# Gate and up projections of paired feed-forward tiles by Strassen's seven products

## The chip, the cores and the metric

The kernel runs on one core of a Trainium2 chip. The core has a matrix engine (PE, with its weight loads shown apart as PEld), a vector engine (DVE), a scalar engine (ACT), a general engine (POOL, which also issues DMAs that add while they write) and a queue engine (SP) that issues the plain DMAs. The metric is the device time of one execution in microseconds; of several executions the median is given.

## The reference

A trunk of two layers over 1024 tokens of width 1024. Layer 0 mixes tokens with a causal convolution module, layer 1 with a causal pooling mixer over windows of 2, 4, 8 and 16 tokens. After each mixer comes a SwiGLU feed-forward of width 2816, and the part that the change touches is its first half:

```
def swiglu_ffn(h, w_gate, w_up, w_down):
    return (jax.nn.silu(h @ w_gate) * (h @ w_up)) @ w_down

h = modulate(rms_norm(x, norm_ffn_g[i]), sh_f, sc_f)
x = x + (1.0 + g_f)[:, None, :] * swiglu_ffn(h, ...)
```

Everything is float32. Shift, scale and gate vectors (the "ada" vectors) come from a product of a conditioning vector with a large matrix for each layer.

## The kernel before, in words

The activations are kept transposed: channels on the 128 partitions, tokens along the free axis. The 1024 tokens are two chunks, A (`ch.i` 0) and B (`ch.i` 1), of 512 tokens. There are therefore four feed-forwards: A and B of layer 0, A and B of layer 1. Each works in 22 tiles `f` of 128 hidden channels.

**Precision.** A float32 factor is split into a high part, rounded to the matrix engine's float32r format, and a low part, the rest. `products` (L406) multiplies high by high, high by low and low by high: three matmuls for each 128 x 128 weight block, each with its own weight load, adding into one PSUM bank. The high part of a weight is an ACT copy of a raw tile that SP's DMA brought (`load_weight`, L391). For the low part ACT writes the negated high part into the second half of the tile and a DMA of POOL's queue adds the raw weight to it from memory. So each weight is fetched twice, and DVE has nothing to do with it.

**Feed-forward.** `ffn_p1` (L790) makes one tile: for gate, then for up, 8 blocks x 3 matmuls of 512 columns; then ACT takes silu of the gate, DVE multiplies with up, ACT casts the high part and DVE or POOL subtracts for the low part. `ffn_p2` (L815) makes the down products of two tiles: for each of 8 output tiles 2 x 3 matmuls, and DVE adds the result, times the gate vector, into the residual `x` (`update`). `ffn` (L827) puts these units in order: a down unit runs after the first tile of the next pair. The last feed-forward ends in `ending` (L844), which makes the down products in two halves of 256 tokens, so that the last norm can start early.

**Order.** PE runs in the order in which the program is written. The other engines are put in order by a list scheduler at compile time, from priorities and estimated times. Background work (the taps of the convolution, norms, the pooling mixer, the layer-1 ada vectors) is written as tasks; `pace` (L175) emits steps of them between matmuls by an estimated clock for each engine, with lower priority than the direct work, and `finish` (L187) emits all that is left of a task where its result is needed. `either` (L141) picks DVE or POOL for an operation by these clocks and the price list `PRICES`.

**Weights.** `run_units` (L526) holds a queue of all weights in order of use and loads ahead as long as fewer than `W_BUFS` = 5 are held. A weight tile is 128 x 2 x 1024 (high and low side by side), and raw weights have 3 buffers.

**Buffers.** `slot` (L227) gives the high and low parts of normalised activations, 16 for each chunk. `wslot` (L231) gives wider tiles, 8 for each chunk; the feed-forward puts its hidden activations in there. `temp` (L252) gives scratch tiles. PSUM has 6 rotating banks and 2 spare ones.

**Around the change.** `with_pool` (L1051) lays the layer-1 pooling of chunk A under the layer-0 feed-forward of B, and the pooling of B under the layer-1 feed-forward of A. It starts the task `pool` at one unit, and at a later unit it waits for it (`need`), emits the pool products (`pool_out`) and starts the norm for the next feed-forward. `final_a`, the last norm of chunk A, runs under the last feed-forward.

Of the kernel before, what the change touches and what calls it, by code (L numbers as in the profile page):

```python
# [16 lines left out]
P = 128  # L17
# [17 lines left out]
GROUP = 2  # L35
W_BUFS = 5
RAW_BUFS = 3
ADA_BUFS = 2
# [8 lines left out]
STRETCH = 1.35  # L47
LATER = 300
DELAY = {"stats": 2.75, "spread": 1.5}
DELAY_BEHIND = {"stats": 8, "spread": 4}  # L50
# [52 lines left out]
def trunk(ctx, tc, xT, c, vec, ada, adan, w1, w2, wgu, wdn, wpl, out):  # L103
# [11 lines left out]

    def matmul(out, lhsT, rhs, start, stop):
        n = out.shape[-1]
        clock["PE"] += n / 2400 * (1 if rhs.dtype == F32R else 4) + 0.0025
        last_mm[0] = nc.tensor.matmul(out, lhsT, rhs, start=start, stop=stop).ins.name  # L119

# [270 lines left out]
    def load_weight(src, n=D, load=nc.sync.dma_start, summed=False):  # L391
        raw = raws.tile([P, D], F32, tag="raw", name=nm("raw"))[:, :n]
        dst = raw if len(src.shape) == 2 else raw.rearrange("p (a b) -> p a b", a=src.shape[1])
        load(dst, src)
        wt = wts.tile([P, 2, D], F32R, tag="w", name=nm("w"))
        S_.copy(wt[:, 0, :n], raw)
        if summed:
            S_.activation(wt[:, 1, :n], raw, AF.Copy, scale=-1.0)
            low = wt[:, 1, :n]
            order(nc.gpsimd.dma_start(low if len(src.shape) == 2 else low.rearrange("p (a b) -> p a b", a=src.shape[1]), src, accum_op=ADD))  # L400
            clock["G"] = max(clock["G"], clock["PE"]) + 1.0
            return wt
        either(n).tensor_tensor(wt[:, 1, :n], raw, wt[:, 0, :n].bitcast(F32), op=SUB)
        return wt

    def products(out, wt, k, act, first, last, o=0, n=None):  # L406

        wk = slice(k * P, (k + 1) * P)
        for i, (wp, a) in enumerate(((0, 0), (0, 1), (1, 0))):
            cols = act[a][:, o : o + n] if n else act[a]  # L410
            matmul(out, wt[:, wp, wk], cols, start=first and i == 0, stop=last and i == 2)

# [113 lines left out]
    def run_units(cap, early):  # L526

        queue = [w for ws, _ in units for w in ws]
        loaded = list(early)
        del queue[: len(early)]  # L530
        used = [0]

        def ahead(free):
            while queue and len(loaded) + used[0] - free < cap:
                loaded.append(load_weight(queue.pop(0), summed=True))
                if len(loaded) > 1:
                    break

        for ws, emit in units:
            def take():  # L540
                ahead(0)
                used[0] += 1
                return loaded.pop(0)
            emit(take)
            used[0] -= len(ws)
            ahead(0)
            pace()
# [278 lines left out]

    def ffn(ch, l, pick, at_end=False):  # L827

        us, pend = [], None
        ends = [NF - n for n in range(0, NF, GROUP)][::-1]  # L830
        if NF % GROUP == 1:
            ends[0] += 1
        for f0, f1 in zip([0] + ends, ends):
# [8 lines left out]
        return us  # L842

    def ending(ch, l, fs):  # L844
# [88 lines left out]
    for k in range(KT + 1):  # L933
        if k < KT:
            w = wts.tile([P, 2, D], F32, tag="w", name=nm("adaw"))
            load_next(w, ada_m[0, k][:, 0:2, :])
            ada_dot(w[:, 1], 0, 1, k)
            tc.add_manual_dep(V_.last.ins, t_last if k else rstd_last, edge, reason="behind the first norm")
# [7 lines left out]
        if k < KT:  # L946
            ada_dot(w[:, 0], 0, 0, k)
            V_.tensor_scalar(scale_m[:, k : k + 1], mod[:, KT + k : KT + k + 1], scale_b[:, k : k + 1], V("norm_mix_g", k), op0=ADD, op1=MUL)
# [101 lines left out]

    def with_pool(us, ch, at, out_at):  # L1051

        for i, (e, ws) in enumerate(us):
            if i == at:
                if ch.i == 0:
                    ada_need((1, 0), (1, 1), (1, 2))
                put(("pool", ch.i), lambda: pool(ch))
            if i == out_at:
# [63 lines left out]
```

## Time and profile before

| what | value |
|---|---|
| median of 3 runs | 1887.41 us (1884.03 to 1890.82) |
| span of the profiled execution, first to last instruction | 1887.1 us |
| busy, share of the span: PE / DVE / ACT / POOL | 96% / 52% / 51% / 34% |
| matmuls on PE | 8104 |
| bytes moved by DMA | 382.31 MB |

The page of the profile gives no separate time of the profiled execution beside its span; the span lies 0.3 us under the median. In the rows of the views, a line number such as L97 or L119 is that of a helper through which all operations of an engine go (L97 for DVE, ACT and POOL, L119 for matmuls), so the names say more than the lines: "gate<-hhi,w" writes the tile `gate` from `hhi` and `w`. In a group row the count stands after x, then the total in us, the mean of one in ns, and the idle time before them with its cause. Durations of matmuls overlap; the distance between their starts is what one costs in a row of many.

### The profile page before, as it was taken

How to read it: one execution, taken by the hardware profiler on the slowest of the kernel's cores; microseconds unless marked ns; L12 is line 12 of the kernel's file. 1: busy time of each engine (PE TensorE's matmuls, PEld its weight loads, DVE VectorE, ACT ScalarE, POOL GpSimd, SP SyncE). 2: the span in 40 equal slices, each digit the busy share in tenths (PEclk: the TensorE clock that was granted, in tenths of full speed). 3: DMA queues.
4: the chain of work that ended last, by engine and by line, in shares of the span. 5: the costliest groups of instructions: out<-in, count | busy, mean ns of one | idle time of the engine just before them, and what ended most of it. 6: DMA issues, size and time to landing. Idle time of an engine off the chain costs nothing.

```text
span 1887.1 us, 21837 instructions
## 1 busy us (share of the span) xinstructions
PE 1803.9 (96%) x8104; PEld 1465.9 (78%) x8104; DVE 985.5 (52%) x1512; ACT 969.5 (51%) x1246; POOL 634.1 (34%) x675
## 2 busy tenths in 40 slices
PE   6899839999999999999999999999999999999996
PEld 4666628788888887888888888888888888888885
DVE  7778872898986326475742224643522243322225
ACT  3655645866666554554454444545544444344443
POOL 3478742687762211264211111321111111111111
PEclk9999969999999999999999999999999999999998
DMA  7968836889798897999978787887887879888782
GB/s 251 296 193 227 211 65 158 206 208 244 199 235 205 210 236 175 249 251 278 270 183 207 173 197 189 194 195 186 189 198 180 198 179 251 179 199 200 180 192 66
DMA packets 115292, 382.31 MB, mean 203 GB/s; under 512 B 11889, under 2 KB 22257, under 8 KB 115186
## 3 DMA queue, kind: packets, MB, share of 16 engines
q0 software_dynamic: 43488, 158.35, 46.0%
q1 hardware_dynamic: 70544, 221.51, 34.6%
q8 instruction: 64, 1.05, 0.2%
q10 hardware_dynamic: 1154, 1.05, 0.2%
q14 instruction: 42, 0.34, 0.1%
HBM read 376.67 MB, written 4.19 MB: 202 GB/s over the span
## 4 chain that ended last, share of the span: by engine, by line
PE 87%; DMA 6%; DVE 5%; issue 1%; ACT 1%; POOL 0%; SPq 0%; DVEq 0%; ACTq 0%
PE dn L119 24%; PE gate L119 24%; PE up L119 23%; PE y L119 6%; DMA adaw<-in_adan_dram 3%; PE a L119 3%; PE g L119 3%; PE first L119 2%; DMA adaw<-in_ada_dram 2%; DVE adaw L97 1%; PE ada L119 1%; DVE x L97 1%; DVE t L97 1%; DVE acc L97 1%; DMA w<-in_wdn_dram 1%
## 5 line engine op out<-in xcount | busy, mean ns | idle before, releaser
L97 ACT CAST w<-raw 128x1024 fp32r<-128x1024 f32 x312 | 326.0, 1045 | 512.0 <-issue 293.9
L119 PE MATMUL gate<-hhi,w 128*128 128x512 f32 x1408 | 451.1, 390 | 0.5 <-DVE x L97 0.5
L119 PE MATMUL up<-hhi,w 128*128 128x512 f32 x1408 | 451.4, 390 | 0.0
L119 PE MATMUL dn<-ghi,w 128*128 128x512 f32 (+1 forms) x1440 | 447.2, 387 | 2.2 <-ACT ghi L97 1.2
L400 POOL DMA_DIRECT2D w<-in_wgu_dram x176 | 154.5, 878 | 760.7 <-ACT w L97 739.0
L97 DVE SCALAR_TENSOR_TENSOR x<-dn,gains,x 128x512 f32<-128x512 f32 (+1 forms) x360 | 261.7, 735 | 119.0 <-PE dn L119 118.7
L97 ACT ACTIVATE w<-raw 128x1024 fp32r<-128x1024 f32 x302 | 319.0, 1056 | 0.0
L119 PEld LDWEIGHTS dn<-ghi,w 128*128 128x128 f32 x1440 | 268.7, 188 | 61.5 <-ACT ghi L97 1.6
L97 DVE TENSOR_TENSOR t<-t,up 128x512 f32<-128x512 f32 x88 | 60.4, 686 | 485.5 <-PE up L119 465.1
L119 PEld LDWEIGHTS gate<-hhi,w 128*128 128x128 f32 x1408 | 264.3, 188 | 56.5 <-DVE x L97 1.0
L119 PEld LDWEIGHTS up<-hhi,w 128*128 128x128 f32 x1408 | 264.3, 188 | 54.7
L119 PE MATMUL dn<-glo,w 128*128 128x512 f32 (+1 forms) x720 | 279.4, 388 | 1.6 <-POOL glo L97 1.6
L119 PE MATMUL gate<-hlo,w 128*128 128x512 f32 x704 | 274.4, 390 | 1.1 <-DVE hlo L97 1.1
L119 PE MATMUL up<-hlo,w 128*128 128x512 f32 x704 | 273.9, 389 | 0.0
L97 POOL TENSOR_TENSOR pa<-pa,pr 128x512 f32<-128x512 f32 x172 | 244.4, 1513 | 19.7 <-ACT pr L97 16.6
L97 DVE SCALAR_TENSOR_TENSOR ca<-u,vecs,ca 128x512 f32<-128x512 f32 x276 | 188.9, 746 | 0.2
L119 PEld LDWEIGHTS dn<-glo,w 128*128 128x128 f32 x720 | 135.5, 188 | 30.0 <-POOL glo L97 1.9
L119 PEld LDWEIGHTS gate<-hlo,w 128*128 128x128 f32 x704 | 132.2, 188 | 29.3 <-DVE hlo L97 1.9
L400 POOL DMA_DIRECT2D w<-in_wdn_dram x88 | 78.2, 889 | 225.3 <-ACT w L97 223.3
L119 PEld LDWEIGHTS up<-hlo,w 128*128 128x128 f32 x704 | 132.2, 188 | 27.2
L97 ACT ACTIVATE t<-gate 128x512 f32<-128x512 f32 x88 | 52.2, 593 | 161.5 <-PE gate L119 155.0
L97 DVE SCALAR_TENSOR_TENSOR adaw<-adaw,cact 128x1024 f32<-128x1024 f32 x64 | 108.4, 1695 | 43.8 <-DMA adaw<-in_ada_dram 42.0
(123 smaller groups left out, 1734.2 us busy)
## 6 DMA issues: line engine op xcount, KB each, us to landing
raw<-in_wgu_dram SPq DMA_DIRECT2D x176, 512.0 KB, 7.1
w<-in_wgu_dram POOLq DMA_DIRECT2D x176, 512.0 KB, 8.0
raw<-in_wdn_dram SPq DMA_DIRECT2D x88, 512.0 KB, 5.4
w<-in_wdn_dram POOLq DMA_DIRECT2D x88, 512.0 KB, 9.4
adaw<-in_ada_dram SPq DMA_DIRECT2D x48, 512.0 KB, 7.5
raw<-in_w_dram SPq DMA_DIRECT2D x44, 512.0 KB, 6.5
w<-in_w_dram POOLq DMA_DIRECT2D x34, 512.0 KB, 8.4
adaw<-in_adan_dram SPq DMA_DIRECT2D x32, 512.0 KB, 5.6
```

The lines of the kernel that those rows point to most:

```text
L97: self.last = self.order(getattr(self.eng, name)(out, *args, **kw))
L119: last_mm[0] = nc.tensor.matmul(out, lhsT, rhs, start=start, stop=stop).ins.name
L400: order(nc.gpsimd.dma_start(low if len(src.shape) == 2 else low.rearrange("p (a b) -> p a b", a=src.shape[1]), src, accum_op=ADD))
```

## The change

In three of the four feed-forwards (B of layer 0, A and B of layer 1), the first two tiles stay as they were. After them come tiles in pairs up to `UNTIL` = (14, 14, 20), and the rest (8, 8 and 2 tiles) as before.

For a pair of tiles `f`, `f+1` the product of the 256 x 1024 weights with the 1024 x 512 activations is cut into halves along all three axes: two tiles, the front and back four channel blocks, and the left and right 256 tokens. That would be 8 quarter products; Strassen's scheme (in Winograd's form) makes it 7 of sums and differences of quarters. An object `Pair` stands for gate or up of such a pair.

- `combined` makes the four sums of activation quarters once for each feed-forward, as a task, with high and low parts, in the other chunk's `slot` tiles.
- `Pair.load` fetches the two raw weights once. `Pair.prepare` makes three plain quarters and four sums, each with high part (ACT) and low part (DVE, or `either`); sums lie in the other chunk's `wslot` tiles. It has a priority of its own, `PREPARED`.
- `ffn_pair` emits seven `quad`s of 4 blocks x 3 matmuls of 256 columns into two PSUM banks. ACT and DVE read a bank between quads that add into the same bank. It prepares the next object midway.
- `Downs` makes the down products of two tiles for 4 of the 8 output tiles, one after every second quad; its weights are fetched once, in halves, and their low parts are subtracted on DVE or POOL.
- Weight tiles are now 9 tiles of 128 x 1024 (high and low each take one), raw tiles 4. `run_units` counts a weight as 2 and a `Pair` as 4 of these 9. In the very first stage two ada loads of 512 KB stand for one of 1024 KB.
- `pooled` starts the pooling task only after the pairs, and needs it at unit `OUT_AT` = 7 of the rest.

```diff
-W_BUFS = 5
-RAW_BUFS = 3
+W_BUFS = 9
+RAW_BUFS = 4
+PREPARED = 120
+UNTIL = (14, 14, 20)
+OUT_AT = 7
...
-        wt = wts.tile([P, 2, D], F32R, tag="w", name=nm("w"))
-        S_.copy(wt[:, 0, :n], raw)
+        hi, lo = (wts.tile([P, D], F32R, tag="w", name=nm("w"))[:, :n] for _ in range(2))
+        S_.copy(hi, raw)
...
+    def combined(ch):
+        other = chunks[1 - ch.i]
+        h = st["h", ch.i]
+        got = st["T", ch.i] = []
+        for k in range(KT // 2):
+            whole = []
+            for hi, lo in (h[k], h[k + KT // 2]):
+                t = window(ch.n, "hf")
+                either(ch.n).tensor_tensor(t, f32(hi), f32(lo), op=ADD)
+                whole.append(t)
+            a, b = whole
+            q12, q34 = temp(ch.n, "tf"), temp(ch.n, "tf")
+            V_.tensor_tensor(q12[:, LEFT], a[:, LEFT], a[:, RIGHT], op=SUB)
+            V_.scalar_tensor_tensor(q12[:, RIGHT], q12[:, LEFT], -1.0, b[:, RIGHT], op0=MUL, op1=SUB)
+            V_.tensor_tensor(q34[:, LEFT], b[:, RIGHT], a[:, RIGHT], op=SUB)
+            V_.scalar_tensor_tensor(q34[:, RIGHT], q12[:, RIGHT], -1.0, b[:, LEFT], op0=MUL, op1=SUB)
+            yield
+            row = []
+            for q in (q12, q34):
+                hi, lo = slot(other, "thi"), slot(other, "tlo")
+                S_.copy(hi, q)
+                V_.tensor_tensor(lo, q, f32(hi), op=SUB)
+                row += [(hi[:, LEFT], lo[:, LEFT]), (hi[:, RIGHT], lo[:, RIGHT])]
+            got.append(row)
+            yield
...
+        def prepare(self):
...
+            with tc.high_priority(offset=-PREPARED):
+                w11 = plain(a11, V_)
+                s1 = temp(QUAD, "acc", 2)
+                V_.tensor_tensor(s1, a21, a22, op=ADD)
+                e1 = summed(s1)
+                s2 = temp(QUAD, "ny", 2)
+                V_.tensor_tensor(s2, s1, a11, op=ADD)
+                e2 = summed(s2)
+                w12 = plain(a12, V_)
+                s3 = temp(QUAD, "acc", 2)
+                V_.tensor_tensor(s3, a11, a21, op=ADD)
+                e3 = summed(s3)
+                s4 = temp(QUAD, "ny", 2)
+                V_.tensor_tensor(s4, s2, a12, op=ADD)
+                e4 = summed(s4)
+                w22 = plain(a22, V_)
...
+    def quad(out, w, acts, first):
+        for k, act in enumerate(acts):
+            cols = slice(k * P, (k + 1) * P)
+            for i, (wp, a) in enumerate(((0, 0), (0, 1), (1, 0))):
+                matmul(out, w[wp][:, cols], act[a], start=first and k + i == 0, stop=k == len(acts) - 1 and i == 2, skip_group_check=True)
...
+    def ffn_pair(ch, l, me, following, downs, later):
...
+            quad(a[:, :H], w11, b11, True)
+            S_.copy(r[:, LEFT], a[:, :H])
+            quad(right, s1, t1, True)
+            S_.copy(q[:, RIGHT], right)
+            pace()
+            down()
+            quad(a[:, :H], s2, t2, False)
+            S_.copy(r[:, RIGHT], a[:, :H])
+            if following is not None and hasattr(following, "raws"):
+                following.prepare()
+            quad(left, w12, b21, False)
+            pace()
+            down()
+            quad(a[:, :H], s3, t3, False)
+            V_.tensor_tensor(q[:, RIGHT], q[:, RIGHT], a[:, :H], op=ADD)
+            quad(right, s4, b22, False)
+            V_.tensor_tensor(r, r, e, op=ADD)
+            if later is not None:
+                later.load(later.dps[0])
+            pace()
+            down()
+            quad(a[:, :H], w22, t4, False)
...
-    fb_, fa_, last = ffn(B, 0, True), ffn(A, 1, True), ffn(B, 1, True, at_end=True)
-    with_pool(fb_[:-1], A, 3, 14)
-    with_pool(fa_[:1] + fb_[-1:] + fa_[1:-1], B, 5, 17)
-    for i, (e, ws) in enumerate(last[:1] + fa_[-1:] + last[1:]):
-        if i == 3:
-            put("final_a", lambda: final(A))
-        unit(e, *ws)
+    before, pairs, rest = ffn_mixed(B, 0, UNTIL[0])
+    put(("T", 1), lambda: combined(B))
+    add(before)
+    paired(B, pairs)
+    pooled(rest[:-1], A, OUT_AT)
+    before, pairs, rest_a = ffn_mixed(A, 1, UNTIL[1])
+    add(before[:1] + rest[-1:])
+    put(("T", 0), lambda: combined(A))
+    add(before[1:])
+    paired(A, pairs)
+    pooled(rest_a[:-1], B, OUT_AT)
+    before, pairs, rest = ffn_mixed(B, 1, UNTIL[2], True)
+    add(before[:1] + rest_a[-1:])
+    put(("T", 1), lambda: combined(B))
+    add(before[1:])
+    put("final_a", lambda: final(A))
+    paired(B, pairs)
+    add(rest)
```

`ffn_mixed` lays out one such feed-forward: the two plain tiles, the pairs with their `Downs`, the left-over `Downs` as units of their own (`alone`) between the first tiles of the rest, and the rest from `ffn`.

More of the change, by code (lines that the diff above doesn't have):

```diff
@@ L410, in products @@
             cols = act[a][:, o : o + n] if n else act[a]
-            matmul(out, wt[:, wp, wk], cols, start=first and i == 0, stop=last and i == 2)
+            matmul(out, wt[wp][:, wk], cols, start=first and i == 0, stop=last and i == 2)
     def rsqrt(v, y, t):
@@ L531, in run_units, with ahead @@
         used = [0]
-        def ahead(free):
-            while queue and len(loaded) + used[0] - free < cap:
-                loaded.append(load_weight(queue.pop(0), summed=True))
+        cost = lambda w: 4 if isinstance(w, Pair) else 2
+        def ahead():
+            held = sum(cost(w) for w in loaded) + used[0]
+            while queue and (held + cost(queue[0]) <= cap or not loaded):
+                w = queue.pop(0)
+                held += cost(w)
+                loaded.append(w.load() if isinstance(w, Pair) else load_weight(w, summed=True))
                 if len(loaded) > 1:
```

185 lines of the change are left out of this document (156 added, 29 removed).

## The prediction

> **What bounds the kernel now.** I read the profile's page first, then busy time by stage, the chain of waits in order of time, single matmuls, and groups by form.
>
> The page: span, engines, and the chain that ended last.
>
> ```profile
> span 1887.1 us, 21837 instructions
> PE 1803.9 (96%) x8104; PEld 1465.9 (78%) x8104; DVE 985.5 (52%) x1512; ACT 969.5 (51%) x1246; POOL 634.1 (34%) x675
> PE 87%; DMA 6%; DVE 5%; issue 1%; ACT 1%; POOL 0%; SPq 0%; DVEq 0%; ACTq 0%
> ```
>
> The three feed-forwards that the change touches run from 754 us to the end; the row 350:650 is inside the first, which is not touched.
>
> ```profile
> 350.00:650.00 300.00, 300.00 (x1327) 247.35 (x1326) 241.90 (x332) 196.26 (x260) 186.73 (x163) 1.00 0.86 216
> 754.00:910.00 156.00, 154.76 (x687) 127.27 (x686) 93.18 (x143) 81.18 (x102) 65.25 (x89) 1.00 0.94 263
> 910.00:1098.00 188.00, 188.00 (x836) 155.32 (x835) 70.66 (x109) 88.89 (x107) 32.64 (x38) 1.00 0.84 204
> 1098.00:1473.00 375.00, 375.00 (x1665) 309.75 (x1664) 150.25 (x223) 181.75 (x222) 80.08 (x91) 1.00 0.82 191
> 1473.00:1857.00 384.00, 384.00 (x1697) 316.93 (x1697) 114.34 (x169) 163.54 (x192) 60.47 (x69) 1.00 0.81 189
> ```
>
> The columns after the stretch are its length and the busy time of PE, PEld, DVE, ACT and POOL, then the granted clock (1.00), DMA share and GB/s. From 910 to 1857 PE never pauses, while DVE is busy 30 to 40% and ACT under 50%. Time there is the number of matmuls times the spacing of their starts. A busy PE says nothing of that spacing, so I take it from the chain of waits (start, length, what):
>
> ```profile
> 1103.71 5.44 PE up L119 x24
> 1109.15 10.99 PE dn L119 x48
> ```
>
> That is 5.44/24 = 226.7 ns for a matmul of 512 columns, and 10.99/48 = 229 ns in the down products. The ending already has matmuls of 256 columns, each with its own weight load. Here is the start of every third, and the group of loads:
>
> ```profile
> 1857.49 0.28 PE L119 MATMUL dn<-glo,w 128*128 128x256 f32 x1
> ...
> 1859.96 0.28 PE L119 MATMUL dn<-glo,w 128*128 128x256 f32 x1
> ```
>
> ```profile
> L119 PEld LDWEIGHTS dn<-ghi,w 128*128 128x128 f32 x1440 | 268.7, 188 | 61.5 <-ACT ghi L97 1.6 <-DMA w<-in_wdn_dram 1.1 <-ACT t L97 0.7
> ```
>
> Between these two starts lie 21 matmuls: 2.47/21 = 117.6 ns. Halving the columns does not quite halve the spacing, and the loads, 188 ns long each, overlap one another.
>
> **The change part by part.**
>
> *Matmuls.* The gate (or up) of two tiles takes 2 x 24 matmuls of 512 columns now, 48 x 226.7 = 10.88 us. By seven quarter products it takes 7 x 4 x 3 = 84 of 256 columns, 84 x 117.6 = 9.88 us. So 1.00 us is saved per pair object. Bounds: if the spacing were half of 226.7 exactly, 84 x 113.4 = 9.52 and 1.36 saved; if the 188 ns of a load were the spacing, 15.8 us and 4.9 lost. I take the measured spacing. `UNTIL` = (14, 14, 20) with the first two tiles left plain gives 6, 6 and 9 pairs of tiles, times gate and up: 42 objects. 42 x 1.00 = **-42.0 us**. Down products in `Downs` are the same 48 matmuls per two tiles.
>
> *Work put on the other engines.* The rows by form (line, engine, operation, count | total, mean ns):
>
> ```profile
> L97 ACT CAST w<-raw 128x1024 fp32r<-128x1024 f32 x312 | 326.0, 1045 | 512.0 <-issue 293.9 <-PE dn L119 86.3 <-PE up L119 58.9
> L97 ACT ACTIVATE w<-raw 128x1024 fp32r<-128x1024 f32 x302 | 319.0, 1056 | 0.0
> L97 DVE SCALAR_TENSOR_TENSOR x<-dn,gains,x 128x512 f32<-128x512 f32 x344 | 254.3, 747 | 117.6 <-PE dn L119 117.3
> L400 POOL DMA_DIRECT2D w<-in_wgu_dram x176 | 154.5, 878 | 760.7 <-ACT w L97 739.0 <-PE dn L119 13.1 <-ACT col L97 5.5
> L97 ACT CAST ghi<-t 128x512 fp32r<-128x512 f32 x88 | 53.2, 605 | 15.0 <-DVE t L97 14.9
> L97 DVE TENSOR_TENSOR acc<-acc,t 128x512 f32<-128x512 f32 x77 | 53.2, 691 | 46.3 <-ACT t L97 41.5 <-ACT acc L97 1.9
> L97 ACT ACTIVATE t<-gate 128x512 f32<-128x512 f32 x88 | 52.2, 593 | 161.5 <-PE gate L119 155.0 <-DVE glo L97 3.3 <-DVE hlo L97 1.9
> L97 POOL TENSOR_TENSOR glo<-t,ghi 128x512 fp32r<-128x512 f32 x24 | 37.1, 1546 | 4.6 <-ACT ghi L97 4.5
> L97 DVE TENSOR_TENSOR acc<-acc,u 128x512 f32<-128x512 f32 x12 | 14.4, 1197 | 0.2
> L97 ACT ACTIVATE x<-x,vecs 128x256 f32<-128x256 f32 x16 | 7.6, 498 | 0.1
> L97 DVE SCALAR_TENSOR_TENSOR x<-dn,gains,x 128x256 f32<-128x256 f32 x16 | 7.4, 480 | 1.4 <-PE dn L119 1.4
> ```
>
> A slot is one pair object with the four down tiles woven in: 9.88 + 24 x 0.229 = 15.4 us of PE (the first object of each phase has no downs). DVE in a slot: three low parts and four sums in `prepare`; of the other four low parts, `either` keeps one by its price list and sends three to POOL; one of two low parts of down weights; and on average one operation of the up epilogue (two operations, up objects only). Those 10 read two SBUF tiles: 6.9 us at 691 ns, 12.0 at the 1197 of the row taken where POOL was busy. With PSUM operands: four updates 3.0, the two sums of quarters 0.48 + 0.69, the two negated products halved 0.5, together 4.7. DVE: **11.6 to 16.7 us against 15.4**. POOL: 4.5 x 1.546 = 7.0 us, 45% of the slot; at that overlap DVE needs 11.6 + 0.45 x 5.1 = 13.9, 90%. ACT: nine casts x 0.605, three copies x 0.498, epilogue 1.4, together 8.3 us. Nothing exceeds 15.4, so their bulk costs nothing as long as PE covers it. The cover is DVE's last 10%; gone, each us over is a us on the end. The accumulating weight DMAs, 878 ns of POOL each, fall away for paired tiles; POOL is off the path, so that gains nothing.
>
> *Waits within a slot.* Quarters 1, 2 and then 3, 5, 7 share banks: before the third product adds into `a`, ACT must have read it; before the fifth, ACT again; before the seventh, DVE. Between lie one quarter product (1.41 us) and one down tile (1.37), 2.8 us for a read of 0.5 us. Queued ahead on ACT or DVE may be operations for the next object, each waiting on the other engine. No row shows this. A wait only adds, so the lower bound is 0; the upper is 2.8 us per slot, lateness of a down tile's and a quarter's length in one handover. I take 0.2 us per object, nearer to nothing because the read is a fifth of its cover: 42 x 0.2 = **+8.4**.
>
> *Weights prefetched less deep.* `W_BUFS` 5 whole tiles becomes 9 halves, and the queue holds 4 weights instead of 5, everywhere, the untouched feed-forward too. While a down unit uses two weights and the next tile's two wait, one free half is left: the low part of the tile after that starts when the down unit ends, one tile (10.88 us) ahead of its use. It needs ACT's 1.056, then POOL's DMA:
>
> ```profile
> w<-in_wgu_dram POOLq DMA_DIRECT2D x176, 512.0 KB, 8.0
> DMA to landing us min/median/max: 5.3/8.3/14.4
> ```
>
> So 1.06 + 8.3 = 9.4 us at the median and 15.5 at worst, against 10.88 + 0.45 (its first use is the third matmul). The cover is there at the median. Behind the waiting matmul stands all of PE. I count 18 such places (10 in the first feed-forward, 8 in the unpaired rests): 0 to 18 x 4.2 = 76; I take 0.3 each, **+5**. The split loads at the start can cost or gain a few us; 0, within -5 to +5.
>
> *The pool mixer pushed together.* It now starts behind the pairs and is needed after 3 tiles, 3 `alone` units and one down unit: 3 x 10.88 + 3 x 5.5 + 11.0 = 60 us. In the second layer's run now, first sum of squares to last low part:
>
> ```profile
> 1172.75 0.68 DVE L97 TENSOR_TENSOR acc<-acc,t 128x512 f32<-128x512 f32 x1
> 1242.42 0.67 DVE L97 TENSOR_TENSOR mxlo<-win,mxhi 128x512 fp32r<-128x512 f32 x1
> 1307.76 10.92 PE y L119 x48
> ```
>
> That is 70 us, and its products came 65 us later, so today it is hidden. Afterwards it is 10 us late if it starts where written and keeps its pace, early if the squares float ahead. 0 to 10 per phase, I take 4, in two phases: **+8**. The norm after it has 5 x 10.88 + 2 x 11 = 76 us and stays hidden.
>
> *Phase starts.* `combined` needs per quarter-row 4 operations of 512 and 4 of 256 columns, 4 x 0.691 + 4 x 0.48 = 4.7, 19 us in all, against at least 22 us of tiles ahead of it or beside it. `prepare` of the first object has no object before it to hide in. 0 to 5 us, I take 1, three times: **+3**.
>
> Sum: -42.0 + 8.4 + 5 + 8 + 3 = -17.6. The profiled execution's span, 1887.1, lies 0.3 under the median of the runs, so I count 0.3 around it: 1887.4 - 17.6 = **1870 us**.
>
> **Rivals.**
> - *All handovers hidden* (the clean case): of the terms only the matmuls are left, 1887.4 - 42.0 = 1845. For it: no wait in any row of 910 to 1857. Against: DVE is at 40% there and near 90% later.
> - *DVE becomes the bound* (slower than before): in the pair slots, two-input operations run at the contended 1197 ns, so a slot lasts 16.7, 1.3 us over PE's 15.4. 42 x 1.3 = 55; with the other terms (16) 1887.4 - 42 + 55 + 16 = 1916. It decides from the point where (15.4 - 11.6)/5.1 = 75% of those operations meet POOL. For it: the row of 1197. Against: POOL's 45%. The Trainium skill, page "SBUF — State Buffer", section "Who interferes with whom", has DVE operations with two SBUF inputs and POOL operations that read SBUF exclude each other, the later waiting whole; the pair of 691 and 1197 agrees, though the 30 to 40% overlap of today cannot tell a lock from a slowdown.
> - *The lateness eats the gain*: about 0.6 us per object instead of 0.2, 25 us in all: 1887.
> - *The weight load becomes the spacing*: 42 x 4.9 = 207 more, 2094. For it: 188 ns is longer than 117.6. Against: the 21 matmuls above ran at 117.6 with such loads. The Trainium skill, page "Perfetto Trace Analysis", section "Identifying the Most-Contended Engine", judges TensorE by the busy share of LDWEIGHTS, which here is 83% and would pass 100%; by that rule this is the outcome. The trace's spacing contradicts it for this load.
>
> **How the numbers follow.** Forecast 45%, clean case 25%, DVE bound 17%, gain eaten 10%, weight load 3%. The likeliest one's own range is 1853 to 1881. The range of 1844 to 1910 takes in the clean case and most of the way to the DVE case. 0.3% (5.7 us) is about what a measurement of this kernel can tell. Faster: 25 + 44 = 69%. Within: 9%, nearly all of the eaten gain. Slower: 17 + 3 and the worse edge of the eaten gain, 22%.
>
> **What would show it.** PE must have 8104 + 42 x 36 = 9616 matmuls, those of 256 columns 117 to 119 ns apart; accumulating loads of gate and up fall from 176 to 92. If the waits of PE in the pair phases are on ACT copies and DVE sums of some 0.2 us, the slot term holds; if DVE is busy over 95% there, the second rival. Waits on `w` DMAs between 350 and 740 show the prefetch term, a gap ahead of the pool products the mixer's. The prediction is wrong if the pair slots' spacing is above 118 ns with no wait in it, or if the untouched part moves by more than 10 us.

## The result and the profile after

The changed kernel takes 1942.98 us (median of 4 runs, 1936.39 to 1947.26) against 1888.61 us before (4 runs): a ratio of 1.0288, interval 1.0263 to 1.0313. It is slower by 54 us, where 1870 us and a gain of 18 was predicted; 1943 lies outside the range. The profiled execution took 1936.39 us, 6.6 below the median, at a span of 1934.6.

Lines of the changed kernel's page, in the order span, busy times, chain of waits by engine, DMA issues:

```profile
span 1934.6 us, 26130 instructions
...
PE 1795.3 (93%) x9616; PEld 1523.1 (79%) x9616; DVE 1341.7 (69%) x2007; ACT 1000.5 (52%) x1546; POOL 909.5 (47%) x807
...
PE 29%; DVE 6%; issue 3%; DMA 1%; POOL 1%; ACT 1%; DVEq 0%; POOLq 0%; ACTq 0%
...
w<-in_wgu_dram POOLq DMA_DIRECT2D x92, 512.0 KB, 8.0
```

The counts are as predicted: 9616 matmuls, 92 accumulating loads of gate and up. PE is busy for 8.6 us less than before, in a span that is 47.5 us longer. So PE waits. (The chain covers less than half of this span and can't serve as a map.)

Busy time by stretch in the changed kernel; columns as in the prediction's rows (length; PE, PEld, DVE, ACT, POOL; granted clock, DMA share, GB/s):

```profile
758.93:780.94 22.01, 14.04 (x86) 12.92 (x84) 19.02 (x27) 9.43 (x18) 12.12 (x9) 0.77 0.46 142
797.00:937.00 140.00, 128.46 (x868) 117.18 (x867) 120.54 (x166) 59.75 (x117) 78.84 (x52) 0.99 0.52 166
997.61:1017.67 20.06, 13.73 (x49) 9.50 (x48) 18.51 (x23) 10.32 (x17) 16.41 (x23) 0.91 0.48 138
1162.79:1188.33 25.54, 13.72 (x85) 12.33 (x84) 20.67 (x31) 11.10 (x21) 13.87 (x9) 0.73 0.28 92
1189.00:1359.00 170.00, 169.97 (x1182) 158.61 (x1182) 116.71 (x164) 83.87 (x158) 82.73 (x67) 1.00 0.37 111
1388.74:1412.33 23.59, 16.63 (x50) 11.29 (x49) 17.59 (x22) 10.64 (x17) 14.56 (x11) 0.71 0.44 124
1557.33:1589.46 32.13, 16.06 (x85) 14.86 (x84) 26.67 (x31) 15.01 (x28) 20.15 (x12) 0.67 0.22 74
1628.00:1865.00 237.00, 236.83 (x1639) 220.30 (x1639) 168.11 (x234) 114.39 (x217) 114.10 (x81) 1.00 0.36 109
```

I call the pair stretches of the three feed-forwards phases 1, 2 and 3. 758.93, 1162.79 and 1557.33 are the starts of their first objects, 997.61 and 1388.74 the starts of left-over down units (`alone`) ahead of the pool products.

- **Phase 2 behind its first object, and phase 3 from 1628 us on, run as the clean case has it**: PE is busy 169.97 of 170 us and 236.83 of 237, with DVE at 69 and 71%.
- **Each first object is far too long**: 84 matmuls in 22.0, 25.5 and 32.1 us.
- **Phase 1 has waits inside its slots** (128.46 of 140), and **two left-over down units together** take 20.1 and 23.6 us for 48 matmuls that took 10.99 before.

Who PE waits for, in the changed kernel from 740 to 1860 us (engine, line, releaser: us in total, times, longest):

```profile
PE gate L122 <- DVE tlo L100: 19.2, 6, 4.5
PE gate L122 <- DVE t L100: 16.8, 6, 5.2
PE dn L122 <- ACT w L100: 7.0, 4, 3.1
PE gate L122 <- ACT t L100: 4.1, 2, 3.0
PE dn L122 <- POOL w L100: 3.8, 3, 2.3
PE up L122 <- DVE t L100: 3.6, 5, 1.2
PE gate L122 <- ACT thi L100: 3.5, 3, 2.5
...
PE dn L122 <- DMA w<-in_wdn_dram: 1.9, 2, 1.0
```

`tlo` and `thi` are the activation sums of `combined`, `t` is the epilogue's scratch (for `gate<-DVE t`, the sum of quarters ahead of the seventh product), `w` a down weight.

**The start of phase 2** on PE's timeline (start, length, what, idle before it with its releaser), with one matmul of the steady part and the same matmul two objects later:

```profile
1169.34 0.58 PE L122 MATMUL gate<-tlo,shi 128*128 128x256 f32 x1 [4.49 <-DVE tlo L100]
...
1173.09 0.58 PE L122 MATMUL gate<-tlo,shi 128*128 128x256 f32 x1 [2.18 <-DVE tlo L100]
1176.37 0.58 PE L122 MATMUL gate<-thi,shi 128*128 128x256 f32 x1 [2.48 <-ACT thi L100]
1179.43 0.58 PE L122 MATMUL gate<-tlo,shi 128*128 128x256 f32 x1 [2.48 <-DVE tlo L100]
...
1740.27 0.28 PE L122 MATMUL gate<-hhi,w 128*128 128x256 f32 x1
...
1771.30 0.28 PE L122 MATMUL gate<-hhi,w 128*128 128x256 f32 x1
```

Every block waits for its sums, and behind each wait a matmul is shown at 0.58 us instead of 0.28, at a granted clock of 0.73 over the object. The first object's 84 matmuls need 84 x 0.119 = 10.0 us; it took 15.5 more, 11.6 of it in these four waits. The other two first objects are not quite alike: in phase 1, 6.0 of 8.0 us of waits are for low parts of the sums (`tlo`); in phase 3 only 4.1 of 16.1, the rest being waits for the sum of quarters on DVE (5.2), for the low part of a weight sum on POOL (3.1) and for ACT (3.7).

The sums on DVE in the changed kernel, with the last idle time ahead of them:

```profile
1140.13 0.69 DVE L100 TENSOR_TENSOR acc<-raw 128x512 f32<-128x512 f32 x1 [10.38 <-DMA raw<-in_wgu_dram]
...
1151.96 0.68 DVE L100 TENSOR_TENSOR hf<-hhi,hlo 128x512 f32<-128x512 f32 x1
...
1158.73 1.78 DVE L100 TENSOR_TENSOR tlo<-tf,thi 128x512 fp32r<-128x512 f32 x1
...
1176.89 0.68 DVE L100 TENSOR_TENSOR w<-raw,w 128x512 fp32r<-128x512 f32 x1
1177.50 0.67 DVE L100 TENSOR_TENSOR t<-t,up 128x512 f32<-128x512 f32 x1
...
1178.70 2.38 DVE L100 TENSOR_TENSOR tlo<-tf,thi 128x512 fp32r<-128x512 f32 x2
```

The sums begin on POOL, then come the first and last rows of phase 1's sums on DVE:

```profile
1145.46 2.83 POOL L100 TENSOR_TENSOR hf<-hhi,hlo 128x512 f32<-128x512 f32 x2
```

```profile
738.20 1.12 DVE L100 TENSOR_TENSOR hf<-hhi,hlo 128x512 f32<-128x512 f32 x1
...
768.36 1.28 DVE L100 TENSOR_TENSOR tlo<-tf,thi 128x512 fp32r<-128x512 f32 x2
```

DVE had stood idle for 10.38 us up to 1140, and used none of that for the sums. POOL begins them at 1145.46 and DVE at 1151.96, when the second plain tile begins (its matmuls start at 1151.87). In phase 3 they begin on POOL at 1536.26, also during the down unit ahead of the second plain tile. The task is put behind that down unit in the program, and in `order` every instruction of a background task gets an edge ("behind the products") to the matmul written last before it. The edge is of the kind `NoSync`: it shapes the order that the list scheduler makes, and the POOL row shows that it makes nothing wait at run time, since the down unit's last matmul starts only at 1151.64.

The work itself was sized rightly. DVE's part of it sums to 18.8, 19.0 and 18.9 us in the three phases, against 19 estimated. But it is spread over 31, 29 and 30 us (738 to 770, 1152 to 1181, 1542 to 1573): low parts of weights, sums for the first object and the tile's epilogue stand between, and the same 128 x 512 operation takes 0.68 or 1.78. Phase 1, whose sums have both plain tiles (21.8 us) beside them, is late for this reason; phases 2 and 3 have only one of the tiles.

**A late seventh product of phase 1**: DVE's timeline, then PE's:

```profile
873.56 1.65 DVE L100 SCALAR_TENSOR_TENSOR adaw<-adaw,cact 128x1024 f32<-128x1024 f32 x1
...
876.41 1.77 DVE L100 TENSOR_TENSOR acc<-raw 128x512 f32<-128x512 f32 x1 [1.19 <-POOL slo L100]
...
882.68 0.41 DVE L100 TENSOR_TENSOR t<-t,gate 128x256 f32<-128x256 f32 x1
```

```profile
883.14 0.39 PE L122 MATMUL gate<-thi,w 128*128 128x256 f32 x1 [2.28 <-DVE t L100]
```

The 0.41 us sum that frees the bank stands on DVE behind products of the layer-1 ada vectors and sums prepared for the next object.

**The account, in spans** (1934.6 against 1887.1, so +47.5). The third feed-forward starts at 737.1 instead of 754.0: -16.9. From there to the end it is 1197.5 instead of 1133.1: +64.4. Steady objects: 31.03 us for two, with their downs, instead of 2 x 10.88 + 10.99 = 32.75, so 0.86 each: 42 x 0.86 = -36. First objects beyond 10.0 us: 12.0 + 15.5 + 22.1 = 49.6. The rest of phase 1: 16.7, of phase 2: 0.5, of phase 3: 11.2 (each phase's length less its matmuls at full spacing). Left-over down units: 9.1 + 12.6 = 21.7. The down units ahead of phases 2 and 3 take 12.2 instead of 11.0 each: 2.5. The ending: 1.8. That makes +68, 4 more than the 64.4. Most of these 4 are in the kernel before too: 1.6 are the last norm's matmuls, which stand inside phase 3 here, and 1.9 are delays that three units of the kernel before have at 821, 833 and 855 us.

### The profile page after: what moved, and what is told of

It is laid out like the page before. It is cut to its first block, busy times and chain, and to the rows that moved or that the text cites. A ratio compares the mean times of both kernels' runs of the same rounds, so it can differ in the third digit from the quotient of the medians.

```text
span 1934.6 us, 26130 instructions
## 1 busy us (share of the span) xinstructions
PE 1795.3 (93%) x9616; PEld 1523.1 (79%) x9616; DVE 1341.7 (69%) x2007; ACT 1000.5 (52%) x1546; POOL 909.5 (47%) x807
## 3 DMA queue, kind: packets, MB, share of 16 engines
q0 software_dynamic: 24480, 89.14, 25.5%
## 5 line engine op out<-in xcount | busy, mean ns | idle before, releaser
L100 ACT CAST w<-raw 128x512 fp32r<-128x512 f32 (+1 forms) x402 | 321.3, 806 | 185.9 <-DMA raw<-in_wdn_dram 75.7
L100 ACT ACTIVATE w<-raw 128x1024 fp32r<-128x1024 f32 x170 | 180.1, 1059 | 302.4 <-PE up L122 80.5
L122 PE MATMUL gate<-hhi,w 128*128 128x512 f32 (+1 forms) x1072 | 305.8, 359 | 0.0
L122 PE MATMUL up<-hhi,w 128*128 128x512 f32 (+1 forms) x1072 | 305.5, 358 | 0.0
L100 POOL TENSOR_TENSOR w<-raw,w 128x512 fp32r<-128x512 f32 (+1 forms) x97 | 142.9, 1473 | 201.0 <-ACT w L100 186.3
L122 PE MATMUL gate<-hlo,w 128*128 128x512 f32 (+1 forms) x536 | 192.3, 359 | 1.1 <-DVE hlo L100 1.1
L122 PE MATMUL up<-hlo,w 128*128 128x512 f32 (+1 forms) x536 | 191.4, 357 | 0.0
L100 POOL TENSOR_TENSOR slo<-acc,shi 128x512 fp32r<-128x512 f32 x84 | 128.9, 1534 | 118.2 <-ACT shi L100 111.1
L100 DVE TENSOR_TENSOR w<-raw,w 128x512 fp32r<-128x512 f32 (+1 forms) x135 | 120.1, 892 | 21.8 <-ACT w L100 21.5
L100 ACT ACTIVATE pr<-u,vecs 128x512 f32<-128x512 f32 x175 | 117.8, 716 | 13.3 <-POOL pa L100 5.9
```

The source lines that it names most:

```text
L100: self.last = self.order(getattr(self.eng, name)(out, *args, **kw))
```

## The experiments

### The early part and the weight pool

**buffers**: the kernel before, with the change's 9 half tiles, 4 raw tiles and split ada loads, no pairs.

```diff
-W_BUFS = 5
-RAW_BUFS = 3
+W_BUFS = 9
+RAW_BUFS = 4
...
-        wt = wts.tile([P, 2, D], F32R, tag="w", name=nm("w"))
+        hi, lo = (wts.tile([P, D], F32R, tag="w", name=nm("w"))[:, :n] for _ in range(2))
...
+            for j in (1, 0):
+                load_next(w[j], ada_m[0, k][:, j, :])
```

> The kernel before with the buffer part of the change alone: nine half weight tiles, four raw tiles, the first ada load in two halves, no paired tiles. Theory (the 17 us by which the third feed-forward part began earlier, 737.1 against 754.0 us, come from the buffers): 1889 - 17 = 1872 us, and the layer-0 feed-forward of B starts its first gate product near 737 us. Rival (they come from the rest of the program being scheduled anew, and four weights held instead of five cost up to 5 us): 1889 to 1894 us, start near 754 us or later.

1883.92 us, ratio 0.9987 [0.9976, 0.9999]. The third feed-forward starts at 739.9 instead of 754.0, but 10 of these 14 us are lost later. **buffers_10_3** is `buffers` with 10 half tiles, the old capacity, and the old 3 raw tiles; against `buffers`:

```diff
-W_BUFS = 9
-RAW_BUFS = 4
+W_BUFS = 10
+RAW_BUFS = 3
```

> The kernel before with half weight tiles and the split first ada load, but ten tiles and three raw ones, so that five weights are held as in the kernel before. Theory (the 10 us that the run with nine tiles lost behind 740 us come from four weights held): the part behind 740 us takes 1133 us again; if the early 14 us come from the halves, 1889 - 14 = 1873 us. Rival (the early 14 us come from the fourth raw tile): start of the third feed-forward near 754 us and 1886 to 1890 us.

1880.94 us, 0.9967 [0.9956, 0.9978]. PE's waits from the third feed-forward on, first of `buffers` (740 to 1840 us), then of `buffers_10_3` (744 to 1840):

```profile
PE dn L119 <- DMA w<-in_wdn_dram: 5.5, 4, 2.5
PE gate L119 <- DMA w<-in_wgu_dram: 1.0, 1, 1.0
```

```profile
PE gate L119 <- DVE x L97: 0.5, 1, 0.5
```

With 10 halves the waits for DMAs are gone and the rest takes 1132.6 us, as before. So the shallower prefetch costs about 10 us, and the early gain, 10 of the 14 us, needs no fourth raw tile.

**ada_split**: before, with only the ada loads of the first stage split.

```diff
-            load_next(w, ada_m[0, k][:, 0:2, :])
+            for j in (1, 0):
+                load_next(w[:, j], ada_m[0, k][:, j, :])
```

> The kernel before, with the first eight ada loads of 1024 KB split into two of 512 KB and nothing else. Theory (the 10 to 14 us that the third feed-forward began earlier come from the split): start near 742 us, 1875 us in all. Rival (they come from the half tiles, which free a high part without its low part): start near 754 us, 1886 to 1890 us.

1887.45 us, 1.0 [0.9984, 1.0015]; the third feed-forward starts at 751.65. Smaller loads alone give at most 2 us of it; the rest comes with the half tiles (half tiles without split loads were not run). In the traces the changed kernel is 2 us ahead when the products `first` end (70.4 against 72.7 us) and 15 us ahead when layer 0's first `y` products begin (263.0 against 277.8), so most of the gain lies in the convolution module. Which tile comes free earlier there stays open.

### One suspect at a time, in the changed kernel

**t_early**: the task of sums is put one plain tile and one down unit earlier in phases 2 and 3; phase 1 stays as it is.

```diff
+    put(("T", 0), lambda: combined(A))
     add(before[:1] + rest[-1:])
-    put(("T", 0), lambda: combined(A))
...
+    put(("T", 1), lambda: combined(B))
     add(before[:1] + rest_a[-1:])
-    put(("T", 1), lambda: combined(B))
```

> The changed kernel with the task of activation sums written one plain tile and one down unit earlier in the second and third paired feed-forward (about 22 us earlier), the first left as it is. Theory (that task is pinned behind the matmul written before it, so at the phase start PE waits for the low parts of the sums): the first paired gate of phases two and three falls from 25.6 and 32.1 us towards 12 and 20 us, the whole to 1943 - 26 = 1917 us. Rival (the first object's own weight sums, waiting for their raw weights, set the start): less than 5 us change, 1938 to 1943 us.

1919.7 us, 1.0171 [1.0153, 1.0189]: 23 us less than the changed kernel. Its first objects of phases 2 and 3 by stretch:

```profile
1170.28:1184.72 14.44, 11.78 (x86) 11.57 (x85) 7.95 (x11) 6.45 (x13) 5.83 (x5) 0.88 0.31 105
1552.84:1566.27 13.43, 10.76 (x85) 10.15 (x84) 12.33 (x12) 6.16 (x13) 10.76 (x8) 1.00 0.34 113
```

25.5 and 32.1 fall to 14.4 and 13.4; phase 1's, not edited, stays (23.5). Where the sums are written in the program is the cause of most of these two starts, phase 3's other waits included. The gain falls short of the 30 us by which they shrank: in this trace the third feed-forward starts 6 us later (743.3), and what follows phase 3's first object takes 6 us longer.

**out_at_9**: the pooling task is needed two units later.

```diff
-OUT_AT = 7
+OUT_AT = 9
```

> The changed kernel with the pooled result needed two units later in the rest of the two feed-forwards that carry pooling (OUT_AT 9, not 7). Theory (the pooling, pinned behind the pairs, is 9 and 13 us late for its products): both down units ahead of the products fall back from 20.1 and 23.6 us to 11.0, the whole to 1943 - 21 = 1922 us. Rival (the wait only moves to the norm behind the products, which has 22 us less cover): no change, 1940 to 1946 us.

1945.85 us, 1.0323 [1.0294, 1.0352], and the two stretches stay at 20.3 and 21.7 us. The theory, mine from the prediction, that the pooling is late and so delays its products, falls. Who PE waits for in that stretch, 1004 to 1027 us in `out_at_9`, and ACT's row in the changed kernel's:

```profile
PE dn L122 <- ACT w L100: 3.2, 2, 2.5
PE dn L122 <- POOL w L100: 2.9, 2, 2.3
```

```profile
1013.26 0.62 ACT L100 CAST w<-raw 128x512 fp32r<-128x512 f32 x1 [4.04 <-PE dn L122]
```

PE waits for down weights, and ACT, which casts them, for PE to give a weight tile back. **alone_apart** puts a plain tile between the two units:

```diff
-        rest[3:3] = [alone(d) for d in theirs[1:]]
+        rest[3:3] = [alone(theirs[1])]
+        rest[(5 if len(rest) > 6 else 4):(5 if len(rest) > 6 else 4)] = [alone(theirs[2])]
```

> The changed kernel with the second and third of the three left-over down units of each paired feed-forward no longer next to each other: a plain tile stands between them. Theory (the 9 and 13 us before the pool products are not the pool's: two left-over units in a row need four half-loads of down weights through what is left of nine weight tiles, each waiting for the one before to be used): both stretches of 20.1 and 23.6 us go back to 11 to 12, the whole to 1943 - 20 = 1923 us. Rival (down weights are late because POOL and DVE do the pooling then): the wait stays, spread over two places, 1938 to 1946 us.

1933.27 us, 1.0241 [1.0212, 1.027]: 10 us less, half of what lay there. The 24 matmuls that still stand where 48 stood take 8.0 and 6.7 us instead of 5.5, and the next down units, 72 matmuls in all, 17.9 and 21.1 instead of 16.5. PE's waits for ACT's casts of down weights, 7.0 us before, fall to 0.6; those for low parts on POOL and DVE (3.8 and 2.4) are then 3.2 and 4.1. So the weight tiles that come back late are the cause of about half; that low parts come late, the rival of the expectation, is what the waits name for the rest, and no run takes that away.

**no_dots**: the layer-1 ada products on DVE are replaced by a copy of one column, so the kernel leaves out layer 1's shift, scale and gate vectors and DVE has that much less to do.

```diff
+        if l == 1:
+            V_.tensor_copy(mod[:, b : b + 1], w[:, 0:1])
+            return
```

> The changed kernel with the 48 DVE products of the layer-1 ada vectors left out: each is replaced by the copy of one column, the loads stay. So layer 1 computes with wrong shift, scale and gate vectors. Theory (in the first paired phase the sum of quarters stands on DVE behind these 1.2 to 1.7 us products, 2.5 us late in most gate objects): the late seventh products of phase one go, 15 us less, 1928 us. Rival (the order of the prepared weight sums alone makes them late): the 2.5 us waits stay, under 4 us change, and then phases two and three would be without waits for another reason.

1930.57 us, 1.023 [1.0208, 1.0251]: 12 us less. PE's waits from 797 to 968 us, in the changed kernel and then in `no_dots`:

```profile
PE gate L122 <- DVE t L100: 9.1, 4, 2.3
PE up L122 <- DVE t L100: 2.5, 4, 1.2
```

```profile
PE up L122 <- ACT t L100: 2.6, 2, 1.4
```

So the ada products in DVE's queue make most of phase 1's slot waits (PE waits 11.6 us there, then 2.6). **dots_early** lets them run ahead of the phase instead:

```diff
-LOAD = {"load": 2.5, "slow": 18.0, "next": 4.0}
+LOAD = {"load": 2.5, "slow": 8.0, "next": 4.0}
```

> The changed kernel with the layer-1 ada products paced 8 us apart, not 18, while the first feed-forward runs, so that nearly all are done before the first pairs. Theory (they alone keep DVE behind in phase one): as with the products left out, the 2.5 us waits of phase one go, 1943 - 12 = 1931 us, with the right result. Rival (more ada loads and DVE work in the first feed-forward delay its weights or the convolution): what phase one gains is lost before 737 us, 1940 to 1950 us.

1936.23 us, 1.0259 [1.0229, 1.0288]. The waits shrink, the feed-forward begins 4 us later (741.4), and phase 1's first object now takes 26.1 us: the work has moved, not gone.

### All together

**all_moved**: `t_early`, `alone_apart` and `dots_early`; also the last norm of A starts behind the ninth object of phase 3, and phase 1 has four plain tiles and their down unit ahead of its pairs.

```diff
+    before, pairs, rest = ffn_mixed(B, 0, UNTIL[0], first=4)
...
-    put("final_a", lambda: final(A))
-    paired(B, pairs)
+    paired(B, pairs[:9])
+    put("final_a", lambda: final(A))
+    add(pairs[9:])
```

> The changed kernel with five moves: activation sums written earlier (phases two and three), left-over down units apart, ada products at 8 us, the last norm of chunk A put behind the ninth object of phase three and not ahead of the first, and phase one with four plain tiles and their first down unit before its pairs (two objects fewer). If the waits are separate, the sum holds: 1943 - 23 - 20 - 12 - 10 - 8 = 1870 us, below the kernel before. Rival (a wait removed only uncovers the next one on DVE, which stays about 75 to 85% busy in the phases): 1890 to 1905 us.

1893.44 us, 1.0033 [1.0018, 1.0049]: 50 us back, but not the 1870 of the theory that these places are all; the rival, that removed waits uncover others, is right. The first objects still take 19.0, 18.0 and 14.2 us, now with 17.6 us of waits for ACT (`gate <- ACT t`), which were 4.1.

**all_final_last**: the same with the last norm of A behind all objects.

```diff
-    add(rest)
+    add(rest[:-1])
+    need("final_a")
+    add(rest[-1:])
```

> As the run with five moves, but the last norm of chunk A behind all objects of phase three and needed before the ending. The two waits of 3.3 and 4.1 us in phase three with their slow clock, 9 us, should go: 1893 - 9 = 1884 us; if the norm only moves its wait into the rest, 1890 to 1896 us.

1886.02 us, 0.9994 [0.9984, 1.0005]: 7 us less, against 9 expected. The norm, started in the middle of phase 3, had cost that.

**late_load**: the same, and the first down weights are loaded at the end of the first object, not midway in it.

```diff
-            if later is not None:
+            if later is not None and downs is not None:
                 later.load(later.dps[0])
...
+            if later is not None and downs is None:
+                later.load(later.dps[0])
```

> As the run all_final_last, with the load and cast of the first down weights of a phase written at the end of the first object, not midway. Theory (at the phase starts ACT's copy of the first quarter stands behind that cast, which waits for its load): the first paired gates fall from 19.0, 18.0 and 14.2 us to 11 to 13, 10 us less than the run all_final_last. Rival (the preparation of the first object itself is late, so that another operation stands there): under 4 us less.

1883.71 us, 0.9984 [0.997, 0.9997]; first objects 18.95, 15.3 and 11.7. In phase 1 the edit moved nothing in ACT's order. ACT's timeline there, then PE's:

```profile
812.38 1.14 ACT L100 CAST w<-raw 128x512 fp32r<-128x512 f32 x2 [5.34 <-DMA raw<-in_wdn_dram]
...
813.95 0.36 ACT L100 COPY t<-gate 128x256 f32<-128x256 f32 x1
```

```profile
814.36 0.58 PE L122 MATMUL gate<-thi,shi 128*128 128x256 f32 x1 [6.92 <-ACT t L100]
```

The copy that frees a bank takes 0.36 us. It stands behind a cast that waits 5.34 us for a raw down weight, and PE waits 6.92 us for it. In the trace this is plain; a run that takes the cast out of that place was not made, so the price rests on this row.

### Other layouts

**p2_first**: `all_moved` in another layout: two plain tiles and their down unit right ahead of the pairs in every phase, no downs woven into the first two objects, and two left-over units instead of three.

```diff
-        before = [ffn_p1(ch, l, f, True, False) for f in range(2)]
+        before = [ffn_p1(ch, l, f, True, False) for f in range(2)] + [ffn_p2(ch, l, [0, 1], True)]
...
-            for at, d in ((2 * i + 1, first), (2 * i + 2, second)):
+            for at, d in ((2 * i + 2, first), (2 * i + 3, second)):
```

> As the run with five moves, but each paired feed-forward makes the down products of its two plain tiles as a whole unit ahead of the pairs (11 us of PE that needs nothing of the pairs), the first two objects carry no down tiles, two left-over down units remain and not three; all three phases start from two plain tiles. Theory (at a phase start ACT's copy of the first quarter stands behind a cast of down weights whose load has not landed, since four raw tiles are shared by the first two objects and the downs): the first paired gates fall from 19.0, 18.0 and 14.2 us to 10 to 12, the whole from 1893 to 1875 us. Rival (objects without down tiles are too short a cover for the preparation of the next, 14 us of DVE against 10 of PE): the waits move to the second and third object, 1885 to 1900 us.

1930.41 us, 1.0231 [1.0212, 1.025]: 30 us above the worse of the two expectations. The first gate now takes 10.07 us in phases 2 and 3, the sums being ready (14.9 in phase 1). But the wait has only changed its place (waits from 740 to 1860 us):

```profile
PE dn L122 <- ACT ghi L100: 18.7, 6, 5.7
PE dn L122 <- DVE glo L100: 7.8, 14, 3.6
PE up L122 <- ACT t L100: 7.2, 5, 2.0
```

A down unit right behind its own tiles waits for their epilogue, and an object without downs has no cover between its quads.

**p2_first_final_last** adds the edit of `all_final_last`:

> As the run p2_first, with the last norm of chunk A behind all objects of phase three, needed before the ending. Theory (that task's eight DVE products of 1.1 us stand ahead of the sums of quarters, 8 us in phase three): 8 us under the run p2_first. Rival (in the short rest it delays the ending by as much): within 3 us of it.

1916.29 us, 1.0156 [1.0133, 1.0179]: 14 us less than `p2_first`, where 8 was expected.

**phase3_only**: pairs in the last feed-forward alone, in the layout of `p2_first`; the two others as before, and the ada products at their old pace.

```diff
-    before, pairs, rest = ffn_mixed(B, 0, UNTIL[0])
...
-    before, pairs, rest_a = ffn_mixed(A, 1, UNTIL[1])
+    fb_, fa_ = ffn(B, 0, True), ffn(A, 1, True)
+    with_pool(fb_[:-1], A, 3, 14)
+    with_pool(fa_[:1] + fb_[-1:] + fa_[1:-1], B, 5, 17)
```

> Pairs in the last feed-forward alone (18 objects, with its down unit first and the norm of A behind the ninth object); the other two as in the kernel before; half tiles as in the change (nine and four). Theory (an object without waits saves 0.8 to 0.9 us, as between the waits of phase two and three: 16.38 us for 48 matmuls of 512 and 24 down matmuls against 15.5): the run with buffers alone took 1884; 1884 - 18 x 0.85 = 1869 plus 3 for the start and 8 for the norm, 1880 us. Rival (more of the objects wait when the phase is scheduled anew): 1885 to 1895 us.

1896.93 us, 1.0054 [1.0037, 1.0072]: in that layout even one phase loses, more than either expectation had.

**last_only**: the same edit on `late_load`: pairs in the last feed-forward alone, sums early, norm behind all objects, left-over units apart, first down weights late. The half tiles stay at 9, and the ada products are again at their old pace.

> Pairs in the last feed-forward alone, laid out as in the run late_load; the other two as in the kernel before; half tiles nine and four. The run phase3_only lost 11 us where the down unit stood right behind its own tiles and 10 at the norm; without both 1897 - 18 = 1879 us. If an object's saving is smaller than 0.85 us, 1884 us, as with the buffers alone.

1876.73 us, 0.9937 [0.9915, 0.9958]: faster than both kernels, by 11 us by the medians against the one before, which is 0.6%. Its first object, the rest of its objects, and the only one of PE's waits from 1500 to 1850 us that is over 0.2 us in total:

```profile
1521.80:1538.24 16.44, 12.81 (x85) 12.61 (x84) 6.96 (x11) 6.44 (x13) 5.85 (x5) 0.79 0.29 93
1538.24:1803.70 265.46, 264.86 (x1839) 246.44 (x1837) 186.38 (x262) 129.88 (x248) 127.92 (x92) 1.00 0.35 107
```

```profile
PE gate L122 <- ACT t L100: 3.8, 2, 3.6
```

Against `buffers`, which differs by these pairs and by the place of the last norm, it gains 7.2 us by the medians: 18 x 0.86 = 15.5 from the objects, less 6.4 at the start, leaves 9. This phase has no ada products beside it and no pooling behind it. `late_load`, with pairs in all three, takes 7 us more; that suggests that pairs in the first two phases cost more than they save even there, but the two runs also differ in the pace of the ada products and in where the pooling lies.

## Why the prediction was wrong

**What bounds the kernel, and the matmul term: right.** The spacing came out at 118 to 119 ns instead of 117.6 (31.03 us for two objects). -36 instead of -42. The prediction asked for 117 to 119 ns and also named a spacing above 118 as a sign of being wrong; the spacing lies on that edge, and what it costs is these 6 us.

**Phase starts: the step that failed.** Predicted +3, measured about 50. I set 19 us of sums against "at least 22 us of tiles ahead of it or beside it". The 19 us were right (18.8 to 19.0 on DVE). The cover was not: in phases 2 and 3 the task is written with only one of the two tiles (10.9 us) beside it and doesn't move ahead to where DVE is idle, and everywhere DVE spreads it over 29 to 31 us among other work, more than the 22 us. `t_early` shows it for phases 2 and 3 (57.7 us of first objects down to 27.9). For phase 1 it is read from the trace; with all moves its start still took 19.0, then waiting for ACT's copy behind the cast of a down weight.

**Pool mixer: right place, wrong cause.** +8 predicted, 21.7 measured at that place. `out_at_9` refutes the mixer; `alone_apart` shows for about half of it the left-over down units starving for weight tiles, which I had not priced: I counted 5.5 us for each. The other half lies in low parts of down weights that come late, by the waits alone.

**Waits within a slot: mis-sized by place.** +8.4 spread evenly; measured about 17 in phase 1, nothing in phase 2 and 11 in phase 3, of which 1.6 are the norm's own matmuls. The mechanism (a read that frees a bank queued behind other work) is the one I named. What I missed is that the length of the queue depends on the background task beside it: ada products (`no_dots`, 12 us), the last norm of A (`all_final_last`, 7 us; 14 in the other layout).

**Prefetch: mechanism right.** +5 predicted; `buffers` loses 10 behind 740 us and `buffers_10_3` none. In the changed kernel, whose pairs take their weights otherwise, two waits for down weights of 1 us each are left. Between 350 and 735 us, where I looked for the most such places, PE waits for no weight at all.

**Early part: missed.** I gave the split loads 0 within 5 either way; the third feed-forward starts 17 us earlier. It comes with the half tiles, as `buffers` shows (14). I had named a shift of over 10 us there as what would prove the prediction wrong, and it did, in the kernel's favour.

**Rivals.** DVE as the bound is wrong: where nothing else is queued, slots last 15.5 us with DVE at 69 to 71%. That its 1916 lies nearer to 1943 than the others is chance. Its row of 1197 ns is a mean: of those twelve operations seven took 0.68 to 0.69 us and five, all beside busy POOL, 0.8 to 3.6. The 1.78 above is of that slow kind, but such operations delayed the sums and did not set the slots. The weight load as the spacing is wrong: with loads busy for 158.61 of 170 us, matmuls start 118 to 119 ns apart. The Trainium skill, "Perfetto Trace Analysis", section "Identifying the Most-Contended Engine", judges by the busy share of LDWEIGHTS, beside the rate of arithmetic, how close TensorE is to its limit. Summed load by load (some 1180 of 0.189 us in these 170 us) that share is 131%, and it doesn't give the spacing: the loads overlap one another. "Lateness eats the gain" had the right kind of cause, but spread it evenly over 42 objects, while most of the cost sits at the seams. The clean case is what phase 2 shows behind its start, and phase 3 from 1628 us on.

What stays open: phase 1's start in full, the low parts of the left-over down weights, the detail of the early gain, and whether pairs in all three phases can win with the old prefetch depth, which was not tried.

## What to carry to other kernels

A scheme that saves 0.86 us per object must be priced at its seams, where an object has no predecessor to hide its preparation: a start that loses 15.5 us eats the gain of 18 objects. Before background work is said to hide, look for what pins it from ahead (where it is written, the place that it gets in an engine's queue) and what stands between its steps, and not only for the time the engine is free. A pool of weight tiles cut from 10 halves to 9 cost 10 us behind 740 us even without the pairs, so buffers given up to a scheme belong into its price.

## What the runs showed of the hardware that I had not expected

In the three first objects of the changed kernel, waits cost PE more than their length. Behind waits of 2 to 5 us matmuls are shown at 0.58 and 0.42 us instead of 0.28, the ones shown at 0.42 start about 213 ns apart instead of 119, and the granted clock over these stretches is 0.77, 0.73 and 0.67. At the start of phase 2, 11.6 us of waiting in four pieces came with 15.5 us of loss.

Smaller tiles of the same bytes shortened the first 754 us by 10 us with no other edit than that and the split loads (`buffers_10_3`), and by 14 with one half tile less and a fourth raw tile (`buffers`), while splitting the loads alone shortened them by 2 (`ada_split`).
